# Last column group: the mean of the last token tile from summed weights, and a rearranged end

## Chip, cores and metric

The kernel runs on one core of a Trainium2 chip. The time is device time in microseconds (us) for one execution, as the median of several; the profile is that of one further execution. Engines are named as the profile does: PE is TensorE, DVE VectorE, ACT ScalarE, POOL GpSimd, SP SyncE, which issues the loads and stores here.

## What is computed

A two-layer decoder trunk over 256 tokens of width 2048: layer 0 is a gated recurrence, layer 1 a sparse attention with three branches. Only the end of layer 1 is touched:

```python
h = x
for i in range(DEPTH):
    ...
    h = _layer_norm(DEEPNORM_ALPHA * h + y, p[-2], p[-1])

def _layer_norm(x, g, b):
    mu = jnp.mean(xf, -1, keepdims=True)
    xc = xf - mu
    var = jnp.mean(xc * xc, -1, keepdims=True)
    return (xc * lax.rsqrt(var + LN_EPS) * g + b)
```

Here y is the product of the gated attention output (256 x 2048) with `l1_w_out` (2048 x 2048). For each token the mean and the variance go over all 2048 columns, so no output column is final before the last product of its row.

## The kernel before

All products are made with float32 values split into a high and a low part (`split`: ACT copies the high part in the reduced type, DVE subtracts it for the low part), three products for each pair of operands: high x high, high x low, low x high. `tok_step` issues these three for 128 tokens and one block of 128 of the 2048 inner rows; its lines are L146, L147 and L148 of the profile.

The output product runs over four groups of 512 columns, c = 0 to 3. The weights of a group come as eight blocks j0 to j7 of 256 inner rows (`load`, 512 KB each, issued by SP into one of four raw buffers `wr`; a buffer is free when its block has been split). `residual` adds ALPHA times the residual `xr` to the product in PSUM (`hb`, L860) and takes the statistics of 256 columns at a time (`stats`, L862). Residual and statistics of group c run while the weights of group c + 1 are split.

Groups 0 to 2 go through both token tiles block by block. The last group goes tile by tile (`project_by_tile`): first token tile 0 with all 512 columns, then tile 1, the last one, with two halves of 256 columns (`halve=True`), each with its own PSUM tile. After each tile `finish` runs: residual and statistics, then `moments` (aggregate L504, epsilon L505, and the power -0.5 on POOL, L232), then for each of four column quarters of 512 a centring (L876: subtract the mean, multiply by the gain) and a scaling (L878: multiply by 1/deviation, add the bias), and the store of the quarter (L879). `manual_schedule` keeps the order on DVE as written within this loop.

The order of everything else on the engines is set by a scheduler at build time, from priorities and its own estimate of the times: it is fixed in the program. So PE takes products of tile 1 in between those of tile 0 where the scheduler saw PE waiting for weights.

Of the kernel before, what the change touches and what calls it, by code (L numbers as in the profile page):

```python
# [8 lines left out]
F32 = mybir.dt.float32  # L9
F32R = mybir.dt.float32r  # L10
I32 = mybir.dt.int32
AF = mybir.ActivationFunctionType
OP = mybir.AluOpType
AX = mybir.AxisListType
# [3 lines left out]
D = 2048  # L18
S = 256
NT = S // 128  # L20
KT = D // 128
KG = KT // 4
DEPTH = 2
ALPHA = (2 * DEPTH) ** 0.25
# [7 lines left out]
AHEAD = 300  # L32
WARM = 8
PT = 2
HOLD = 7
# [20 lines left out]
def trunk(ctx, tc, a, out):  # L56
    nc = tc.nc
    pe, act, dve, pool = nc.tensor, nc.scalar, nc.vector, nc.gpsimd
    x = a["x"].rearrange("o s d -> (o s) d")
    xt = a["xT"].rearrange("(k p) s -> p k s", p=128)  # L60
    y = out.rearrange("o s d -> (o s) d")
# [9 lines left out]
    def pjb(shape):  # L71
        return pj.tile(shape, F32, name="pjb", tag="pjb")

    def mxb(shape):
        return mx.tile(shape, F32, name="mxb", tag="mxb")

    def split(hi, lo, src):

        act.activation(hi, src, AF.Copy)  # L79
        dve.tensor_tensor(lo, src, hi.bitcast(F32), op=OP.subtract)  # L80
# [22 lines left out]
    def load(w, j, c0, n):  # L103

        raw = slot([128, 2, n], F32, "wr", 3, 1)
        nc.sync.dma_start(raw, w[256 * j:256 * (j + 1), c0:c0 + n].rearrange("(k p) n -> p k n", p=128))
        return raw

    def weights(w, j, c0, n):
        return parts(load(w, j, c0, n))  # L110
# [7 lines left out]
    def widen():  # L118
        extra[0] = wide.enter_context(tc.tile_pool(name="wide", bufs=3, side="right"))
# [7 lines left out]
    def slot(shape, dtype, name, n, more):  # L127

        turn[name] = i = (turn.get(name, -1) + 1) % (n + more)
        p, b = (extra[0], more) if extra[0] and i >= n else (wts, n)  # L130
        if spare[0] and name == "wr" and extra[0] is None:

            spare[1] = i = (spare[1] + 1) % (n + SPARE)
            p, name, b = (spare[0], "ws", SPARE) if i >= n else (wts, name, n)
        return p.tile(shape, dtype, name=name, tag=name, bufs=b)

    def parts(raw):
        hi = slot(list(raw.shape), F32R, "wh", 5, 3)
        lo = slot(list(raw.shape), F32R, "wl", 5, 3)
        with tc.high_priority(AHEAD):  # L140
            split(hi, lo, raw)
        return hi, lo

    def tok_step(ps, xs, k, t, wh, wl):
        xh, xl = xs.at(k, slice(128 * t, 128 * (t + 1)))
        pe.matmul(ps, xh, wh, start=(k == 0), stop=False)  # L146
        pe.matmul(ps, xh, wl, start=False, stop=False)  # L147
        pe.matmul(ps, xl, wh, start=False, stop=(k == KT - 1))  # L148
# [10 lines left out]
                also(j)  # L159
        return ps  # L160

    def project_by_tile(xs, w, c0, after, behind=None, halve=False):


        ws = [weights(w, j, c0, 512) for j in range(KT // 2)]
        for t in range(NT):

            n = 256 if halve and t == NT - 1 else 512
            ps = []
            for c in range(0, 512, n):  # L170
                ps.append(pjb([128, n]))
                for k in range(KT):
                    hi, lo = ws[k // 2]
                    with tc.issue_after(behind) if behind and k >= HOLD else nullcontext():
                        tok_step(ps[-1], xs, k, t, hi[:, k % 2, c:c + n], lo[:, k % 2, c:c + n])
            behind = after(t, ps if len(ps) > 1 else ps[0])
        return behind

    def project_t(xs, w, c0, before=None, also=None):
# [20 lines left out]
    def transposed(src):  # L200

        ps = mxb([128, 4, 128])
        for i in range(4):
            last[0] = pe.transpose(ps[:, i], src[:, i], ident).ins  # L204
        return ps
# [6 lines left out]
    halves = consts.tile([128, 16], F32, name="halves")  # L212
# [18 lines left out]
    def rsqrt(o, v):  # L231
        pool.tensor_tensor(o, v, halves[:, :v.shape[1]], op=OP.pow)  # L232
# [88 lines left out]
    with tc.tile_pool(name="start", bufs=4) as start:  # L321
# [3 lines left out]
        ps = mxb([128, 128])  # L325
# [32 lines left out]
    oT = Pair("b")  # L358
# [116 lines left out]
    with tc.tile_pool(name="m0", bufs=1) as m0:  # L475
        ad = m0.tile([128, NT, 4, 128], F32, name="ad")
        pool.memset(ad, 0.0)
        for g in range(4):
            c0 = 512 * g
# [4 lines left out]
            v = m0.tile([128, NT, 512], F32, name="v")  # L484
# [16 lines left out]
    def moments(p, hb, stats, t):  # L501

        mv = p.tile([128, 4], F32, name="mv")
        dve.bn_aggr(mv[:, 0:2], stats[:, t])  # L504
        dve.tensor_scalar(mv[:, 2:3], mv[:, 1:2], LN_EPS, None, op0=OP.add)  # L505
        rsqrt(mv[:, 3:4], mv[:, 2:3])
        return mv

    hT = Pair("a")
    with tc.tile_pool(name="n0", bufs=2) as n0:  # L510
        hb = n0.tile([128, NT, D], F32, name="hb", bufs=1)
        stats = n0.tile([128, NT, 4, 6], F32, name="stats", bufs=1)
        for c in range(4):
            cs = slice(512 * c, 512 * (c + 1))
            xr = n0.tile([128, NT, 512], F32, name="xr")
            nc.gpsimd.dma_start(xr, x[:, cs].rearrange("(t p) d -> p t d", p=128))

            def residual(t, ps, c=c, cs=cs, xr=xr):
                dve.scalar_tensor_tensor(hb[:, t, cs], xr[:, t], ALPHA, ps, op0=OP.mult, op1=OP.add)
                dve.bn_stats(stats[:, t, c], hb[:, t, cs])  # L520

            def finish(t, ps):
                residual(t, ps)
                mv = moments(n0, hb, stats, t)
                for g in range(KG):
                    h = hb[:, t, 512 * g:512 * (g + 1)]
                    dve.tensor_scalar(h, h, mv[:, 0:1], mv[:, 3:4], op0=OP.subtract, op1=OP.mult)
                    ps = transposed(h.rearrange("p (k d) -> p k d", d=128))
                    h1 = n0.tile([128, 4, 128], F32, name="h1")
                    for k in range(4):  # L530
                        n = 4 * g + k
                        act.activation(h1[:, k], ps[:, k], AF.Identity, scale=g0c[:, n:n + 1],
                                       bias=b0c[:, n:n + 1])
                    hT.put(g, t, h1)
                nc.gpsimd.dma_start(norm0[128 * t:128 * (t + 1), :], hb[:, t])
                return last[0]
# [11 lines left out]
    oT = Pair("b")  # L548
# [79 lines left out]
    with tc.tile_pool(name="cmp", bufs=1) as cp:  # L628
# [38 lines left out]
        steps = []  # L667
# [16 lines left out]
        h = ck.hidden()  # L684
        ps = mxb([128, 4, NB])
# [9 lines left out]
        n = (512 + 48) // 2  # L695
        for t, ps in enumerate(project(hT, w1, C_VW, step, n=n)):
            split2(vals, (slice(None), t, 1, slice(0, n)), ps)
        h = cv.hidden()
# [5 lines left out]
        ps = mxb([128, 4, 128])  # L704
# [4 lines left out]
        ps = ps.rearrange("p g d -> p (g d)")  # L709
        for i in range(2):  # L710
            r, o = (slice(64 * b, 64 * b + 64) for b in (i, 1 - i))
# [111 lines left out]
    n1 = ctx.enter_context(tc.tile_pool(name="n1", bufs=2))  # L823
    hb = n1.tile([128, NT, D], F32, name="hb", bufs=1)
    stats = n1.tile([128, NT, 8, 6], F32, name="stats", bufs=1)
# [17 lines left out]
        return r  # L843


    for c in range(4):
        cs = slice(512 * c, 512 * (c + 1))

        xr = []

        def behind(j, c=c, xr=xr):
            if j == 3:
                xr.append(fetch(c))

        def residual(t, ps, c=c, xr=xr, parts=range(2)):
            xr = xr[0]
            n = ps.shape[1] // len(parts)
            for i, u in enumerate(parts):
                h = hb[:, t, 512 * c + 256 * u:512 * c + 256 * (u + 1)]
                dve.scalar_tensor_tensor(h, xr[:, t, 256 * u:256 * (u + 1)], ALPHA, ps[:, n * i:n * (i + 1)],  # L860
                                         op0=OP.mult, op1=OP.add)
                dve.bn_stats(stats[:, t, 2 * c + u], h)  # L862

        def finish(t, ps):
            if t:
                for u in range(2):
                    residual(t, ps[u], parts=(u,))
            else:
                residual(t, ps)
            mv = moments(n1, hb, stats, t)  # L870
            with tc.manual_schedule(engines={mybir.EngineType.DVE}):
                for g, half in ((0, 0), (0, 1), (1, 0), (1, 1), (2, 0), (2, 1), (3, 0), (3, 1)):
                    gs = slice(512 * g, 512 * (g + 1))
                    h = hb[:, t, gs]
                    if half == 0:
                        dve.scalar_tensor_tensor(h, h, mv[:, 0:1], g1[:, gs], op0=OP.subtract, op1=OP.mult)  # L876
                        continue
                    dve.scalar_tensor_tensor(h, h, mv[:, 3:4], b1[:, gs], op0=OP.mult, op1=OP.add)  # L878
                    nc.sync.dma_start(y[128 * t:128 * (t + 1), gs], h)  # L879

        if c < 3:
            for t, ps in enumerate(project(oT, a["l1_w_out"], 512 * c, behind)):
                residual(t, ps)
            if c == 2:
                last_xr = fetch(3)
            if c == 1:
                widen()
                g1, b1 = row("l1_ln_g"), row("l1_ln_b")
        else:
            xr.append(last_xr)  # L890
            project_by_tile(oT, a["l1_w_out"], 512 * c, finish, halve=True)
    wide.close()


# [31 lines left out]
```

## Time and profile before

| | us |
|---|---|
| median of 3 runs (1012.67 to 1014.42) | 1012.85 |
| the profiled execution | 1013.42 |
| its span, first to last instruction | 1011.7 |
| busy in the span: PE / DVE / ACT / POOL | 995.0 / 670.4 / 544.2 / 117.4 |

PE is busy 98% of the span, in matrix products that are issued one behind the other; a product's length in the timeline is longer than the distance to the next, because they overlap. For the distance between two operations compare their starts. All times in the rows are counted from the span's start.

### The profile page before, as it was taken

The numbers are of one execution on the slowest core, as the hardware profiler recorded it, in microseconds if no ns is written. First come the engines' busy times: TensorE is split into PE (matmuls) and PEld (weight loads), VectorE is DVE, ScalarE is ACT, GpSimd is POOL, SyncE is SP. The second block draws the span as 40 slices with busy tenths as digits, with TensorE's granted clock in tenths as the row PEclk, the third lists the DMA queues.
The fourth block names the chain that finished last, engine by engine and source line by source line (L and its number), as shares of the span: only waits on it lengthen the run. The fifth ranks groups of instructions, "written<-read, shape, count | busy, mean of one in ns | idle before, by whom it ended". The sixth has DMA issues, their size and how long they took to land.

```text
span 1011.7 us, 15913 instructions
## 1 busy us (share of the span) xinstructions
PE 995.0 (98%) x6041; PEld 883.0 (87%) x6041; DVE 670.4 (66%) x1101; ACT 544.2 (54%) x864; POOL 117.4 (12%) x180
## 2 busy tenths in 40 slices
PE   8999999999999999999999999999999999999995
PEld 8988998899889988888889888999989889998775
DVE  6796668656765677656575665555858568775566
ACT  6654455444544554434386655554857667774240
POOL 0400300030002000310011020101020022000540
PEclk9999999999999999999999999999999999999998
DMA  8875565556555665557466776666454455346962
GB/s 296 258 228 160 150 181 173 161 154 187 167 166 157 175 180 153 161 168 267 136 217 231 231 238 218 173 207 170 126 166 143 145 150 151 116 143 179 321 237 83
DMA packets 100780, 185.25 MB, mean 183 GB/s; under 512 B 6096, under 2 KB 20512, under 8 KB 100192
## 3 DMA queue, kind: packets, MB, share of 16 engines
q1 hardware_dynamic: 99232, 178.67, 57.4%
q0 software_dynamic: 1472, 5.56, 1.7%
q8 instruction: 47, 0.77, 0.3%
q14 instruction: 29, 0.24, 0.1%
HBM read 180.02 MB, written 4.19 MB: 182 GB/s over the span
## 4 chain that ended last, share of the span: by engine, by line
PE 91%; DMA 3%; DVE 2%; issue 1%; POOL 1%; SPq 0%; ACT 0%; POOLq 0%; DVEq 0%; ACTq 0%
PE pjb L147 17%; PE pjb L148 17%; PE pjb L146 17%; PE pjb L191 10%; PE pjb L193 10%; PE pjb L194 10%; PE mxb L431 2%; DMA wr<-in_l_w_out_dram 2%; PE mxb L204 1%; PE mxb L554 1%; PE mxb L556 1%; PE mxb L555 1%; PE mxb L785 1%; DVE wl L80 1%; DMA gb<-in_l_ln_g_dram 1%
## 5 line engine op out<-in xcount | busy, mean ns | idle before, releaser
L80 DVE TENSOR_TENSOR wl<-wr,wh 128x1024 fp32r<-128x1024 f32 (+2 forms) x305 | 369.5, 1217 | 197.8 <-ACT wh L79 195.8
L79 ACT ACTIVATE wh<-wr 128x1024 fp32r<-128x1024 f32 (+2 forms) x305 | 316.7, 1043 | 314.0 <-PE pjb L148 163.7
L191 PE MATMUL pjb<-ah,wh 128*128 128x256 f32 x832 | 236.0, 284 | 1.5 <-ACT wh L79 1.5
L193 PE MATMUL pjb<-al,wh 128*128 128x256 f32 x832 | 236.2, 285 | 0.0
L194 PE MATMUL pjb<-ah,wl 128*128 128x256 f32 x832 | 234.5, 284 | 0.5 <-DVE wl L80 0.5
L147 PE MATMUL pjb<-wl,ah 128*128 128x512 f32 (+1 forms) x576 | 222.6, 387 | 0.0
L146 PE MATMUL pjb<-wh,ah 128*128 128x512 f32 (+1 forms) x576 | 222.4, 387 | 0.0
L148 PE MATMUL pjb<-wh,al 128*128 128x512 f32 (+1 forms) x576 | 222.3, 386 | 0.0
L191 PEld LDWEIGHTS pjb<-ah,wh 128*128 128x128 f32 x832 | 157.4, 189 | 2.4 <-ACT wh L79 1.9
L194 PEld LDWEIGHTS pjb<-ah,wl 128*128 128x128 f32 x832 | 156.5, 189 | 0.9 <-DVE wl L80 0.7
L193 PEld LDWEIGHTS pjb<-al,wh 128*128 128x128 f32 x832 | 156.6, 188 | 0.5
L148 PEld LDWEIGHTS pjb<-wh,al 128*128 128x128 f32 x576 | 108.7, 189 | 22.2
L146 PEld LDWEIGHTS pjb<-wh,ah 128*128 128x128 f32 x576 | 108.7, 189 | 21.8
L147 PEld LDWEIGHTS pjb<-wl,ah 128*128 128x128 f32 x576 | 108.7, 189 | 21.3
L147 PE MATMUL pjb<-wl,bh 128*128 128x512 f32 (+1 forms) x272 | 105.1, 386 | 1.3 <-DVE wl L80 1.3
L148 PE MATMUL pjb<-wh,bl 128*128 128x512 f32 (+1 forms) x272 | 104.2, 384 | 0.0
L146 PE MATMUL pjb<-wh,bh 128*128 128x512 f32 (+1 forms) x272 | 103.2, 384 | 0.9 <-ACT wh L79 0.9
L147 PEld LDWEIGHTS pjb<-wl,bh 128*128 128x128 f32 x272 | 51.3, 189 | 13.7 <-DVE wl L80 3.1
L146 PEld LDWEIGHTS pjb<-wh,bh 128*128 128x128 f32 x272 | 51.1, 189 | 12.3 <-ACT wh L79 1.8
L148 PEld LDWEIGHTS pjb<-wh,bl 128*128 128x128 f32 x272 | 51.4, 189 | 10.4
L494 POOL TENSOR_TENSOR gz<-gz,gn 128x512 f32<-128x512 f32 x8 | 13.6, 1695 | 317.1 <-ACT gz L493 316.6
L80 DVE TENSOR_TENSOR wl<-ws,wh 128x1024 fp32r<-128x1024 f32 (+1 forms) x25 | 27.0, 1090 | 18.5 <-ACT wh L79 18.4
(222 smaller groups left out, 1047.4 us busy)
## 6 DMA issues: line engine op xcount, KB each, us to landing
wr<-in_l_w_in_dram SPq DMA_DIRECT2D x218, 512.0 KB, 3.8
wr<-in_l_w_out_dram SPq DMA_DIRECT2D x64, 512.0 KB, 4.4
ws<-in_l_w_in_dram SPq DMA_DIRECT2D x12, 512.0 KB, 4.5
wr<-in_l_cmp_w_k_dram SPq DMA_DIRECT2D x5, 512.0 KB, 3.9
wr<-in_l_cmp_w_v_dram SPq DMA_DIRECT2D x5, 512.0 KB, 3.8
wr<-in_l_w_in_dram SPq DMA_DIRECT2D x9, 280.0 KB, 3.1
xr<-in_x_dram POOLq DMA_DIRECT2D x4, 512.0 KB, 5.3
norm<-hb POOLq DMA_DIRECT2D x2, 1024.0 KB, 5.5
```

The lines of the kernel that those rows point to most:

```text
L79: act.activation(hi, src, AF.Copy)
L80: dve.tensor_tensor(lo, src, hi.bitcast(F32), op=OP.subtract)
L146: pe.matmul(ps, xh, wh, start=(k == 0), stop=False)
L147: pe.matmul(ps, xh, wl, start=False, stop=False)
L148: pe.matmul(ps, xl, wh, start=False, stop=(k == KT - 1))
L191: pe.matmul(o, hi[:, kk, c], xh, start=(k == 0 and b % 2 == 0), stop=False, skip_group_check=True)
L193: pe.matmul(o, hi[:, kk, c], xl, start=False, stop=False, skip_group_check=True)
L194: pe.matmul(o, lo[:, kk, c], xh, start=False, stop=(k == KT - 1), skip_group_check=True)
L204: last[0] = pe.transpose(ps[:, i], src[:, i], ident).ins
L431: pe.matmul(ps[:, h], km[:, h].rearrange("p b r j -> p (b r j)"), later, start=True, stop=True)
L494: pool.tensor_tensor(z, z, gn, op=OP.mult)
L554: pe.matmul(o, a[0], b[0], start=start, stop=False)
```

## The change

Three things are changed, all in the last column group.

The weights of this group get two more columns. For each block DVE sums the 256 columns of the second half (`tensor_reduce`, L864); the sum is split into high and low like the weights and stands, twice, behind the first half, so a row of a block is 256 + 2 + 256 columns with a stride of 258 between the halves. Token tile 0 reads the two halves as one operand of 2 x 256 columns; the last tile's first half reads 258 columns, its second 256. Column 256 of the first half's product is then the sum over the second half's columns of the product, one number for each token.

From it the mean of the last tile is known when its first half is done (`me`): the mean of the 1792 columns that are in `hb` by then (aggregate of seven statistics), the sum of the residual's last 256 columns, and the product's column 256.

With this mean the quarters are centred ahead of the variance: quarters 0 and 1 before the second half's residual, quarters 2 and 3 (the latter as two halves) behind `moments`' first two steps; then the four scalings and their stores follow. The variance is still that of `moments` over all eight statistics. Tile 0 is finished as before.

```diff
-    def project_by_tile(xs, w, c0, after, behind=None, halve=False):
+    def project_by_tile(xs, w, c0, after, behind=None, summed=None):
...
         for t in range(NT):
-
-            n = 256 if halve and t == NT - 1 else 512
...
+            if summed and t == NT - 1:
+                after(t, steps(pjb([128, 258]), t, 2), steps(pjb([128, 256]), t, 4))
+            else:
+                behind = after(t, steps(pjb([128, 512]), t, 0, behind))
         return behind
...
+    def summed(raw):
+
+
+        parts = [slot([128, 2, 516], F32R, name, 5, 3) for name in ("wh", "wl")]
+        ws = n1.tile([128, 2], F32, name="ws")
+        with tc.high_priority(AHEAD):
+            split(*(bass.AP(tensor=v.tensor, offset=v.offset, ap=[v.ap[0], [516, 2], [258, 2], [1, 256]])
+                    for v in parts), raw.rearrange("p k (u n) -> p k u n", u=2))
+            dve.tensor_reduce(ws, raw[:, :, 256:512], axis=AX.X, op=OP.add)
+            split(*(v[:, :, 256:258] for v in parts), ws[:, :, None].to_broadcast([128, 2, 2]))
...
+        def finish(t, ps, other=None):
...
+            known = D - 256
+            me = n1.tile([128, 6], F32, name="me", bufs=1)
+            dve.tensor_reduce(me[:, 0:1], xr[0][:, t, 256:512], axis=AX.X, op=OP.add)
             with tc.manual_schedule(engines={mybir.EngineType.DVE}):
...
+                residual(t, ps[:, 0:256], parts=(0,))
+                dve.scalar_tensor_tensor(me[:, 1:2], me[:, 0:1], ALPHA, ps[:, 256:257], op0=OP.mult, op1=OP.add)
+                dve.bn_aggr(me[:, 2:4], stats[:, t, 0:7])
+                dve.tensor_scalar(me[:, 4:5], me[:, 1:2], 1.0 / D, None, op0=OP.mult)
+                dve.scalar_tensor_tensor(me[:, 5:6], me[:, 2:3], known / D, me[:, 4:5], op0=OP.mult, op1=OP.add)
+                centred(t, me[:, 5:6], *quarters[0:2])
+                residual(t, other, parts=(1,))
+                mv = moments(n1, hb, stats, t)
+                centred(t, me[:, 5:6], quarters[2], (1536, known), (known, D))
+                scaled(t, mv[:, 3:4], *quarters)
```

The order of the instructions is the program's, engine by engine. First DVE where the weights of the last group are split. Before, from block j4 on (`wl_9810`) to j7 (`wl_9828`); `hb` and `stats` are residual and statistics of group c = 2:

```order
L80 TENSOR_TENSOR wl_9810<-wr_9807,wh_9809 128x1024
L860 SCALAR_TENSOR_TENSOR hb_9276<-xr_9685,pjb_9611 128x256 x2
L860 SCALAR_TENSOR_TENSOR hb_9276<-xr_9685,pjb_9612 128x256 x2
L80 TENSOR_TENSOR wl_9816<-wr_9813,wh_9815 128x1024
L862 BN_STATS stats_9277<-hb_9276 128x6 x4
L80 TENSOR_TENSOR wl_9822<-wr_9819,wh_9821 128x1024
L80 TENSOR_TENSOR wl_9828<-wr_9825,wh_9827 128x1024
```

In the changed kernel, the same place from the split of j4 (`wl_9826`) to that of j7 (`wl_9856`); `ws` are the sums:

```order
L80 TENSOR_TENSOR wl_9826<-wr_9823,wh_9825 128x4x256
L80 TENSOR_TENSOR wl_9816<-ws_9817,wh_9815 128x2x2
L887 SCALAR_TENSOR_TENSOR hb_9276<-xr_9685,pjb_9611 128x256 x2
L864 TENSOR_REDUCE ws_9827<-wr_9823 128x2
L887 SCALAR_TENSOR_TENSOR hb_9276<-xr_9685,pjb_9612 128x256 x2
L80 TENSOR_TENSOR wl_9836<-wr_9833,wh_9835 128x4x256
L864 TENSOR_REDUCE ws_9837<-wr_9833 128x2
L889 BN_STATS stats_9277<-hb_9276 128x6 x2
L80 TENSOR_TENSOR wl_9846<-wr_9843,wh_9845 128x4x256
L80 TENSOR_TENSOR wl_9826<-ws_9827,wh_9825 128x2x2
L889 BN_STATS stats_9277<-hb_9276 128x6 x2
L80 TENSOR_TENSOR wl_9856<-wr_9853,wh_9855 128x4x256
```

The sums of j4 and j5 stand ahead of the splits of j5 and j6; those of j6 and j7 follow behind the last split, ahead of the residual of token tile 0.

Second PE, at the first place where a product of the last tile is taken in between those of tile 0. Before (`pjb_9831` is tile 0, `pjb_9903` the last tile's first half) it stands behind the first product of j6:

```order
L146 MATMUL pjb_9831<-wh_9821,bh_5007 128x512
L146 MATMUL pjb_9903<-wh_9785,bh_5004 128x256
L147 MATMUL pjb_9903<-wl_9786,bh_5004 128x256
L148 MATMUL pjb_9903<-wh_9785,bl_5008 128x256
L146 MATMUL pjb_9903<-wh_9785,bh_5004 128x256
L147 MATMUL pjb_9903<-wl_9786,bh_5004 128x256
L147 MATMUL pjb_9831<-wl_9822,bh_5007 128x512
```

In the changed kernel (`pjb_9863` is tile 0, `pjb_9935` the first half with its two sums) it stands behind the first product of j5:

```order
L146 MATMUL pjb_9863<-wh_9835,bh_5006 128x512
L146 MATMUL pjb_9935<-wh_9785,bh_5004 128x258
L147 MATMUL pjb_9935<-wl_9786,bh_5004 128x258
L148 MATMUL pjb_9935<-wh_9785,bl_5008 128x258
L146 MATMUL pjb_9935<-wh_9785,bh_5004 128x258
L147 MATMUL pjb_9935<-wl_9786,bh_5004 128x258
L148 MATMUL pjb_9935<-wh_9785,bl_5008 128x258
L147 MATMUL pjb_9863<-wl_9836,bh_5006 128x512
```

Before, these five are all; in the changed kernel five more stand behind the first product of j6 and six behind that of j7, 17 together.

Third DVE at the end, from the last scaling of tile 0 on. Before:

```order
L878 SCALAR_TENSOR_TENSOR hb_9276<-hb_9276,mv_9884,l1_ln_b_9609 128x512
L860 SCALAR_TENSOR_TENSOR hb_9276<-xr_9774,pjb_9952 128x256
L862 BN_STATS stats_9277<-hb_9276 128x6
L504 BN_AGGR mv_10005<-stats_9277 128x2
L505 TENSOR_SCALAR mv_10005<-mv_10005 128x1
L876 SCALAR_TENSOR_TENSOR hb_9276<-hb_9276,mv_10005,l1_ln_g_9607 128x512
L878 SCALAR_TENSOR_TENSOR hb_9276<-hb_9276,mv_10005,l1_ln_b_9609 128x512
```

The last two rows come four times. In the changed kernel:

```order
L919 BN_AGGR me_10033<-stats_9277 128x2
L920 TENSOR_SCALAR me_10033<-me_10033 128x1
L899 SCALAR_TENSOR_TENSOR hb_9276<-hb_9276,mv_9916,l1_ln_b_9609 128x512
L921 SCALAR_TENSOR_TENSOR me_10033<-me_10033 128x1
L894 SCALAR_TENSOR_TENSOR hb_9276<-hb_9276,me_10033,l1_ln_g_9607 128x512 x2
L887 SCALAR_TENSOR_TENSOR hb_9276<-xr_9774,pjb_9984 128x256
L889 BN_STATS stats_9277<-hb_9276 128x6
L514 BN_AGGR mv_10047<-stats_9277 128x2
L515 TENSOR_SCALAR mv_10047<-mv_10047 128x1
L894 SCALAR_TENSOR_TENSOR hb_9276<-hb_9276,me_10033,l1_ln_g_9607 128x512
L894 SCALAR_TENSOR_TENSOR hb_9276<-hb_9276,me_10033,l1_ln_g_9607 128x256 x2
L899 SCALAR_TENSOR_TENSOR hb_9276<-hb_9276,mv_10047,l1_ln_b_9609 128x512 x4
```

The known mean and two centrings have moved ahead of the second half's residual (L887), the other centrings stand behind the epsilon (L515), and the four scalings come in a row.

## Rows read from the trace of the kernel before

**Rows 1.** Chain of waits of the whole span: shares of the engines.

```profile
PE 91%; DMA 3%; DVE 2%; issue 1%; POOL 1%; SPq 0%; ACT 0%; POOLq 0%; DVEq 0%; ACTq 0%
```

**Rows 2.** Stretches: length, busy PE, PEld, DVE, ACT, POOL, clock, DMA share, GB/s.

```profile
975.00:985.00 10.00, 9.16 (x37) 6.41 (x36) 8.69 (x13) 5.40 (x6) 0.68 (x1) 1.00 0.69 225
...
989.70:1000.40 10.70, 10.69 (x91) 10.48 (x89) 8.07 (x16) 0.00 (x0) 1.01 (x1) 1.00 0.26 99
1000.40:1008.10 7.70, 0.00 (x0) 0.00 (x0) 7.02 (x12) 0.00 (x0) 0.98 (x1) 0.67 0.25 97
1008.10:1011.70 3.60, 0.00 (x0) 0.00 (x0) 0.01 (x1) 0.00 (x0) 0.00 (x0) 0.50 0.22 85
```

**Rows 3.** Timeline of DVE behind the last product: start, length, operation, [idle before].

```profile
1000.43 0.42 DVE L860 SCALAR_TENSOR_TENSOR hb<-xr,pjb 128x256 f32<-128x256 f32 x1 [2.09 <-PE pjb L148]
...
1001.34 0.37 DVE L504 BATCH_NORM_AGGREGATE mv<-stats 128x2 f32<-128x48 f32 x1
1001.75 0.15 DVE L505 TENSOR_SCALAR mv<-mv 128x1 f32<-128x1 f32 x1
1001.82 0.74 DVE L876 SCALAR_TENSOR_TENSOR hb<-hb,mv,l_ln_g 128x512 f32<-128x512 f32 x1
1003.00 0.75 DVE L878 SCALAR_TENSOR_TENSOR hb<-hb,mv,l_ln_b 128x512 f32<-128x512 f32 x1 [0.44 <-POOL mv L232]
1003.67 0.75 DVE L876 SCALAR_TENSOR_TENSOR hb<-hb,mv,l_ln_g 128x512 f32<-128x512 f32 x1
1004.45 0.75 DVE L878 SCALAR_TENSOR_TENSOR hb<-hb,mv,l_ln_b 128x512 f32<-128x512 f32 x1
...
1007.35 0.75 DVE L878 SCALAR_TENSOR_TENSOR hb<-hb,mv,l_ln_b 128x512 f32<-128x512 f32 x1
```

**Rows 4.** Timeline of DVE at the splits of j1 to j4.

```profile
975.57 5.24 DVE L80 TENSOR_TENSOR wl<-wr,wh 128x1024 fp32r<-128x1024 f32 x4 [5.92 <-ACT wh L79]
```

**Rows 5.** Timeline of PE: a wait for a split, and the last two products.

```profile
983.33 0.50 PE L147 MATMUL pjb<-wl,bh 128*128 128x512 f32 x1 [0.61 <-DVE wl L80]
...
999.99 0.28 PE L147 MATMUL pjb<-wl,bh 128*128 128x256 f32 x1
1000.11 0.28 PE L148 MATMUL pjb<-wh,bl 128*128 128x256 f32 x1
```

**Rows 6.** Timeline of DVE at the end of token tile 0.

```profile
989.70 0.75 DVE L860 SCALAR_TENSOR_TENSOR hb<-xr,pjb 128x256 f32<-128x256 f32 x2 [1.67 <-PE pjb L148]
...
992.83 0.75 DVE L878 SCALAR_TENSOR_TENSOR hb<-hb,mv,l_ln_b 128x512 f32<-128x512 f32 x1 [0.46 <-POOL mv L232]
```

**Rows 7.** Timeline of DVE in the attention: a split, two reduces, a small operation.

```profile
841.26 1.23 DVE L80 TENSOR_TENSOR wl<-wr,wh 128x1024 fp32r<-128x1024 f32 x1 [0.70 <-ACT wh L79]
842.40 1.27 DVE L749 TENSOR_REDUCE st<-p 128x2 f32<-128x512 f32 x2
843.59 0.17 DVE L738 TENSOR_TENSOR p<-mxb,cmask 128x16 f32<-128x16 f32 x1
843.67 0.41 DVE L743 TENSOR_TENSOR p<-mxb,tri 128x256 f32<-128x256 f32 x1
```

**Rows 8.** ACT's groups by shape, a small one: busy us, mean ns, idle before.

```profile
L764 ACT ACTIVATE pcs<-p 128x64 fp32r<-128x64 f32 x16 | 3.8, 246 | 0.0
```

**Rows 9.** Timeline of PE in the attention: products of 272 columns.

```profile
842.72 0.29 PE L554 MATMUL mxb<-keys,qT 128*128 128x272 f32 x1
842.85 0.29 PE L555 MATMUL mxb<-keys,qT 128*128 128x272 f32 x1
```

**Rows 10.** Bytes moved in 40 slices of 1004.0 to 1011.7 us.

```profile
GB/s 0 0 0 266 426 372 287 11 0 0 74 372 415 383 117 0 0 0 245 404 404 298 11 0 0 74 362 372 426 128 0 0 0 0 0 0 0 0 0 0
```

**Rows 11.** The load of j7: issue, landing of such loads, ACT's copy.

```profile
979.52 0.37 SPq L106 DMA_DIRECT2D wr<-in_l_w_out_dram  x1
...
wr<-in_l_w_out_dram SPq DMA_DIRECT2D x8, 512.0 KB, 7.0
...
985.71 1.06 ACT L79 ACTIVATE wh<-wr 128x1024 fp32r<-128x1024 f32 x1 [0.27 <-DMA wr<-in_l_w_out_dram]
```

More of the change, by code (lines that the diff above doesn't have):

```diff
@@ L160, in project, with steps @@
         return ps
-    def project_by_tile(xs, w, c0, after, behind=None, halve=False):
-        ws = [weights(w, j, c0, 512) for j in range(KT // 2)]
-        for t in range(NT):
-            n = 256 if halve and t == NT - 1 else 512
[L169 to L176, printed above, removed]
+    def project_by_tile(xs, w, c0, after, behind=None, summed=None):
+        ws = []
+        for j in range(KT // 2):
+            if summed:
+                ws.append(summed(load(w, j, c0, 512)))
+            else:
+                hi, lo = weights(w, j, c0, 512)
+                ws.append([(hi[:, kk], lo[:, kk]) for kk in range(2)])
+        def steps(ps, t, i, behind=None):
+            for k in range(KT):
+                hi, lo = ws[k // 2][k % 2][i:i + 2]
+                with tc.issue_after(behind) if behind and k >= HOLD else nullcontext():
+                    tok_step(ps, xs, k, t, hi, lo)
+            return ps
+        for t in range(NT):
+            if summed and t == NT - 1:
+                after(t, steps(pjb([128, 258]), t, 2), steps(pjb([128, 256]), t, 4))
+            else:
+                behind = after(t, steps(pjb([128, 512]), t, 0, behind))
         return behind
@@ L843, in row, with halves @@
         return r
+    def summed(raw):
[6 more added lines that the diff above has]
+            split(*(v[:, :, 256:258] for v in parts), ws[:, :, None].to_broadcast([128, 2, 2]))
+        def halves(v, kk):
+            return bass.AP(tensor=v.tensor, offset=v.offset + 516 * kk, ap=[v.ap[0], [258, 2], [1, 256]])
+        return [[halves(v, kk) for v in parts] + [v[:, kk, 0:258] for v in parts] +
+                [v[:, kk, 258:514] for v in parts] for kk in range(2)]
     for c in range(4):
@@ L862, in residual, with centred @@
                 dve.bn_stats(stats[:, t, 2 * c + u], h)
[L864 to L868, printed above, removed]
-                residual(t, ps)
-            mv = moments(n1, hb, stats, t)
-            with tc.manual_schedule(engines={mybir.EngineType.DVE}):
[L872 to L879, printed above, removed]
+        def centred(t, m, *parts):
+            for a, b in parts:
+                h = hb[:, t, a:b]
+                dve.scalar_tensor_tensor(h, h, m, g1[:, a:b], op0=OP.subtract, op1=OP.mult)
@@ new lines, in scaled @@
+        def scaled(t, r, *parts):
+            for a, b in parts:
+                h = hb[:, t, a:b]
+                dve.scalar_tensor_tensor(h, h, r, b1[:, a:b], op0=OP.mult, op1=OP.add)
+                nc.sync.dma_start(y[128 * t:128 * (t + 1), a:b], h)
+        def finish(t, ps, other=None):
+            quarters = [(512 * g, 512 * (g + 1)) for g in range(4)]
+            if not t:
+                residual(t, ps)
+                mv = moments(n1, hb, stats, t)
+                with tc.manual_schedule(engines={mybir.EngineType.DVE}):
+                    for q in quarters:
+                        centred(t, mv[:, 0:1], q)
+                        scaled(t, mv[:, 3:4], q)
+                return
+            known = D - 256
+            me = n1.tile([128, 6], F32, name="me", bufs=1)
+            dve.tensor_reduce(me[:, 0:1], xr[0][:, t, 256:512], axis=AX.X, op=OP.add)
+            with tc.manual_schedule(engines={mybir.EngineType.DVE}):
+                residual(t, ps[:, 0:256], parts=(0,))
[5 more added lines that the diff above has]
+                residual(t, other, parts=(1,))
+                mv = moments(n1, hb, stats, t)
+                centred(t, me[:, 5:6], quarters[2], (1536, known), (known, D))
+                scaled(t, mv[:, 3:4], *quarters)
@@ L890, in trunk @@
             xr.append(last_xr)
-            project_by_tile(oT, a["l1_w_out"], 512 * c, finish, halve=True)
+            project_by_tile(oT, a["l1_w_out"], 512 * c, finish, summed=summed)
     wide.close()
```

## The prediction

> **What bounds the kernel now.** I read the chain of waits first. TensorE (PE) carries 91% of it [rows 1]; nothing upstream of the last column group is touched by the change, so only the tail matters. Next the stretches: until 1000.4 us PE is nearly full, then it has nothing left, and VectorE (DVE) alone works 7.7 us, followed by 3.6 us in which the last store lands and the program ends [rows 2]. The timeline of DVE shows what those 7.7 us are: residual and statistics of the last 256 columns (1000.43), aggregate (1001.34), epsilon (1001.75), and then four pairs "centre, scale", the first of which waits for GpSimd's power [rows 3]. Last, the stage before: the weights of the last group are split as they land (DVE 975.57, at the pace of ACT and the loads), and PE waits for them now and then, for instance 0.61 us at 983.33 [rows 4, 5]. So DVE has slack in that stage, but less than it seems: PE's idle time there is mostly a wait for DVE or for what feeds it.
>
> Names: j0 to j7 are the eight weight blocks of the last group, t0 and t1 its two token tiles; t1 is the last tile, t1a and t1b its column halves. R is the time at which DVE starts the residual of t0 (989.70 now), r1 that of the residual of t1b (1000.43 now).
>
> **What leaves the end.** After r1 DVE now needs 1000.43 to 1007.35 + 0.75 = 1008.10, that is 7.67 us [rows 3]. In the change, residual, statistics, aggregate and epsilon stay: 1000.43 to 1001.82, 1.39 us. Then come the centring of 512 and of twice 256 columns, and four scalings in a row. A 512-wide operation that does not need the one ahead starts 0.67 us behind it (1003.00 to 1003.67), one that does 0.78 us (1003.67 to 1004.45) [rows 3]; a 256-wide one takes 0.33 (0.75 for two, 0.42 for one) [rows 6, 3]. So the first scaling could start at 1.39 + 0.67 + 0.33 + 0.33 = 2.72 us. GpSimd's power is ready 1003.00 - 1001.75 = 1.25 us behind the epsilon [rows 3], at 1.32 + 1.25 = 2.57: hidden by 0.15 us behind the three centrings (without this cover it would still cost nothing, since the centrings end later). Scalings: 3 x 0.67 + 0.75 = 2.76. End at 5.48 us behind r1 instead of 7.67: **2.19 us less**, if r1 stays.
>
> [...]
>
> **What is added in front.** On DVE 22 operations more, all in the last group; on ACT eight small copies, between the block copies.
>
> First the weight stage. DVE's order for j2 to j7 becomes: sum over 512 numbers (tensor reduce), split of the block, small split of the two sums, and in between the residuals and statistics of the group before (four 256-wide operations of each kind, as now). j0's sum runs while the next loads are awaited, and j1's before its block is split (it needs the load alone, the split ACT's copy too), so both are hidden by the idle time ahead of 975.57, 5.92 us [rows 4]. From 975.57 on I add: seven splits x 1.14 (841.26 to 842.40) = 7.98; six sums x 0.595 (843.59 - 842.40 for two) = 3.57; seven small splits x 0.08 (843.59 to 843.67; the nearest is 16 wide, these are 4) = 0.56 [rows 7]; eight 256-wide x 0.33 = 2.64; the sum of the 256 residual columns 0.33. Together 15.08: DVE would be through at 990.65. The last sums go through ACT and back (a 64-wide ACT operation takes 0.246 us, a small split 0.17, and the reduce's own end trails by 0.08 [rows 7, 8]), so I add 0.4: **R = 991.05**, 1.35 later than now. The split reads and writes rows that are 258 apart instead of one run of 1024; no row shows that, I take it at nothing (the upper bound is two operations of 512 for one of 1024, 7 x 0.2 = 1.4 us).
>
> ACT keeps up: eight times 0.25 more in a stage where it stands idle between loads. PE can't go ahead of this: its second product of each block needs DVE's low half. But its order puts 17 products of t1a where it now has 5 (the order stands with the change), 12 x 0.119 = 1.43 us that fill the longer waits; t0 then ends at about 990.9, and what is left of t1, 79 products, takes 79 x 0.119 = 9.4 us. The work of PE is the same but for 48 x 2 columns: 272 columns take 0.13 (842.72 to 842.85) [rows 9], 256 take 0.119, so 48 x 0.001 = 0.05 us. I keep PE's end at 1000.4 (last product at 1000.11 [rows 5]), with 0.3 either way.
>
> Then from R to r1. Now: R to the first scaling 992.83 - 989.70 = 3.13 [rows 6]. In the change the same 3.13, and until r1 nine 512-wide operations (four scalings and three centrings of t0, two centrings of t1) x 0.67 = 6.03, residual and statistics of t1a 2 x 0.33 = 0.66, and the known mean: an aggregate (0.37) and three one-column operations, 0.37 + 3 x 0.07 + some 0.1 for waits among them = 0.65 (1001.34 to 1001.75 to 1001.82 [rows 3]). Sum 10.47: **r1 = 991.05 + 10.47 = 1001.52**, 1.1 us after PE is done. Before, DVE reached this place early and waited for PE; now PE waits for nobody and DVE is late. That is the cost: 1.1 of the 2.19 us.
>
> DVE ends at 1001.52 + 5.48 = 1007.0 instead of 1008.10: **-1.1 us**. The four stores of t1 then follow each other at 0.67 instead of 1.45 us. The bytes of a store move in a burst of about 0.83 us (four to five slices of 7.7 / 40 = 0.19 us, the full ones at 370 to 430 GB/s) [rows 10]; 262 KB at 390 GB/s need 0.67, so between nothing and 3 x 0.16 = 0.5 us of queueing. I take 0.1, because the rate within a burst matches the pace. What follows DVE's end, 3.6 us [rows 2], stays. The profiled execution took 1013.42 (span 1011.7 and 1.7 around it); the sum gives 1012.4 for it, and as it lies 0.57 above the median of 1012.85 shown, **1012.85 - 1.0 = 1011.9**.
>
> **Rivals.**
> - *DVE is not late.* If the weight stage and the known mean cost 1.1 us less than my sum, r1 waits for PE again at 1000.43 and the whole 2.19 comes, less 0.1 for stores: 1010.75. For it: the splits might overlap better than 1.14. Against: every price is a measured pitch, and the small splits have ACT in their loop.
> - *The gain is eaten by a late load.* The load of j7 goes out when DVE is through with j3: 979.52 now, about 980.7 then, since three sums stand ahead (behind it on SP's queue stand only the stores, which come much later). It is landed when ACT starts on it, 985.71, 6.2 us later; the median of these loads is 7.0 [rows 11]. With 6.2 it lands at 986.9, ACT's copy ends at 988.0, and DVE comes to it at 988.1: just covered. It decides from 7 us on; at 8 us R moves by 1.7 and the sum is +0.7: 1013.5. The same result comes if the strided split costs its upper bound (+0.4: 1013.2). Together this case is 1012.6 to 1013.9, a gain not to be seen.
> - *Slower: TensorE dislikes the new operands.* t0's products read two runs of 256 columns with a gap, t1a's read 258 columns. If 258 columns took two passes, 2 x 0.119, 48 products would cost 5.8 us more, PE would end at 1006.2, and DVE 5.48 later: +3.6, 1016.4. It decides for slower (over 0.2%) when PE ends 4.2 us later, 0.04 us on each of 96 products. Against: 272 and 256 columns stand in proportion [rows 9, 5].
>
> **How the numbers follow.** 0.2% is 2.0 us, about what a measurement of this kernel tells from no change. The forecast (1011 to 1012.5): 0.58. DVE not late: 0.11, of which some lies below 1010.8. Late load or split: 0.23. Slow operands: 0.08. Faster by over 0.2% 0.10, within 0.82, slower 0.08. The range leaves out the slow operands and the fringe of the best case: 1010.8 to 1013.6.
>
> **What the new profile would show.** Right: DVE without a gap from about 976 to the end; its residual of t0 at 991 +- 0.5; the residual of t1b over 0.8 us after PE's last product; 5.5 us from there to DVE's end, with no wait for GpSimd; stores 0.67 apart. Wrong: DVE waiting for PE at r1 (best case), for ACT or a load in 980 to 989 (late load), or 258-wide products more than 0.125 us apart.

## The result and the profile after

| | before | after |
|---|---|---|
| median, us (6 runs each) | 1013.02 (1012.67 to 1014.42) | 1005.55 (1005.22 to 1006.60) |
| ratio, 95% interval | | 0.993 [0.992, 0.994] |
| the profiled execution | 1013.42 | 1005.65 |
| its span | 1011.7 | 1003.9 |

The change gains 7.5 us where 1.0 was forecast; 1005.55 lies well below the range of 1010.8 to 1013.6. The end of the program went nearly as the prediction had it, but began 7 us earlier. First the page of the changed kernel, its head and the busy times:

```profile
span 1003.9 us, 15938 instructions
...
PE 988.1 (98%) x6041; PEld 877.3 (87%) x6041; DVE 675.4 (67%) x1123; ACT 545.3 (54%) x872; POOL 118.1 (12%) x180
```

DVE has 22 operations and 5.0 us more, as the change says. PE has the same 6041 products and 6.9 us less (995.0 before). Nothing in the diff shortens a product; the last group's are even a little wider.

The prediction named the timeline of DVE as its test; here it is, in the weight stage and behind it:

```profile
968.74 1.23 DVE L80 TENSOR_TENSOR wl<-wr,wh 128x1024 fp32r<-128x1024 f32 x1 [0.49 <-ACT wh L79]
...
982.39 1.27 DVE L864 TENSOR_REDUCE ws<-wr 128x2 f32<-128x512 f32 x2
983.58 0.15 DVE L80 TENSOR_TENSOR wl<-ws,wh 128x4 fp32r<-128x4 f32 x1
983.93 0.17 DVE L80 TENSOR_TENSOR wl<-ws,wh 128x4 fp32r<-128x4 f32 x1 [0.20 <-ACT wh L79]
984.19 0.75 DVE L887 SCALAR_TENSOR_TENSOR hb<-xr,pjb 128x256 f32<-128x256 f32 x2
...
994.47 0.41 DVE L887 SCALAR_TENSOR_TENSOR hb<-xr,pjb 128x256 f32<-128x256 f32 x1
...
995.85 1.53 DVE L894 SCALAR_TENSOR_TENSOR hb<-hb,me,l_ln_g 128x512 f32<-128x512 f32 x3
997.30 2.73 DVE L899 SCALAR_TENSOR_TENSOR hb<-hb,mv,l_ln_b 128x512 f32<-128x512 f32 x4
```

And PE's last product:

```profile
993.33 0.28 PE L148 MATMUL pjb<-wh,bl 128*128 128x256 f32 x1
```

The reader is to see two things. From one row to the next the distances are the forecast ones: 15.45 us from j1's split to R (968.74 to 984.19), 10.28 from R to r1 (994.47), 5.56 from r1 to the end of the four scalings (997.30 + 2.73); no wait for POOL ahead of the scalings, where [rows 3] has one of 0.44. But the first of these rows stands 6.83 us ahead of its place in [rows 4] (975.57).

So I went upstream, to a load that stands ahead of the last groups in SP's queue, before and after:

```profile
931.62 1.41 SPq L842 DMA_DIRECT2D l_ln_b<-in_l_ln_b_dram  x1
```

```profile
924.57 1.39 SPq L852 DMA_DIRECT2D l_ln_b<-in_l_ln_b_dram  x1
```

It goes out 7.05 us earlier, though every instruction ahead of it is the same in the same order. What follows it takes 80.1 us before (1011.7 - 931.62) and 79.3 after. So **7 of the 7.8 us between the two spans came from a part of the program that the diff doesn't touch.** Two stretches show how. Each reaches from one product to another, the same two in both kernels; the first has 238 products of 256 columns between the starts, the second 224 of 512 (the count in the row includes one or two more at the edges). The rows are those of stretches: length, busy time of PE, clock, DMA share, GB/s. Before, and after:

```profile
230.41:258.96 28.55, 28.55 (x240) 1.00 0.64 185
448.93:501.40 52.47, 52.47 (x225) 1.00 0.62 201
```

```profile
228.46:256.77 28.31, 28.31 (x240) 1.00 0.62 186
445.45:497.58 52.13, 52.13 (x226) 1.00 0.61 202
```

PE waits for nothing in either and has its full clock. Yet the pitch of the products, from one start to the next (length by 238 and by 224), is 120.0 ns before and 118.9 after with 256 columns, 234.2 and 232.7 with 512. At the first stretch the changed kernel is 1.95 us ahead, at the second 3.48, at the load above 7.05: the gain grows over the whole program. What the change does to all of it is one thing: a buffer of a tag in a tile pool is as large as the largest tile asked of that tag, and the last group's `wh` and `wl` ask for 2x516 elements. So every buffer of the split weights in the main pool (`wts`; for most of the program an extra pool, `wide`, adds three buffers of each tag) takes 4128 bytes of a partition in place of 4096, from the first instruction on, and all these tiles lie elsewhere.

### The profile page after: what moved, and what is told of

Same layout as the page of the kernel before. It is cut to its first block, busy times and chain, and to the rows that moved or that the text cites. A ratio compares the mean times of both kernels' runs of the same rounds, so it can differ in the third digit from the quotient of the medians.

```text
span 1003.9 us, 15938 instructions
## 1 busy us (share of the span) xinstructions
PE 988.1 (98%) x6041; PEld 877.3 (87%) x6041; DVE 675.4 (67%) x1123; ACT 545.3 (54%) x872; POOL 118.1 (12%) x180
## 3 DMA queue, kind: packets, MB, share of 16 engines
q0 software_dynamic: 1472, 5.56, 1.7%
## 4 chain that ended last, share of the span: by engine, by line
PE 90%; DMA 4%; DVE 3%; POOL 1%; issue 1%; ACT 1%; SPq 0%; DVEq 0%; POOLq 0%
PE pjb L146 16%; PE pjb L148 16%; PE pjb L147 16%; PE pjb L201 10%; PE pjb L204 10%; PE pjb L203 10%; PE mxb L441 2%; DMA wr<-in_l_w_out_dram 2%; DMA gb<-in_l_ln_g_dram 1%; PE mxb L214 1%; PE mxb L564 1%; PE mxb L565 1%; PE mxb L566 1%; PE mxb L795 1%; DVE wl L80 1%; PE mxb L614 1%
## 5 line engine op out<-in xcount | busy, mean ns | idle before, releaser
L147 PE MATMUL pjb<-wl,bh 128*128 128x512 f32 (+2 forms) x272 | 104.5, 385 | 2.2 <-DVE wl L80 1.9
L148 PE MATMUL pjb<-wh,bl 128*128 128x512 f32 (+2 forms) x272 | 103.6, 382 | 0.0
L146 PE MATMUL pjb<-wh,bh 128*128 128x512 f32 (+2 forms) x272 | 102.6, 383 | 0.3 <-ACT wh L79 0.3
L80 DVE TENSOR_TENSOR wl<-ws,wh 128x1024 fp32r<-128x1024 f32 (+2 forms) x33 | 28.2, 863 | 18.4 <-ACT wh L79 18.2
```

## Experiments

In the kernel before, the allocation puts all split-weight tiles at 480 past a multiple of 512 bytes, 4096 apart, and the activations that they are multiplied with (`ah`, `al`, `bh`, `bl`) at 64. In the changed kernel the main pool's split weights lie at 160 to 448, each 32 past the one before, and the extra pool's nearly all at 160. The operands of nearly all products start a multiple of 512 bytes into their tiles, so these numbers hold for them as well. The distance below is from the activations' place to the weights': 416 before.

The medians of before in the three rounds of runs were 1012.14, 1012.85 and 1012.65 us; each kernel is compared with that of its own round.

**The larger buffers alone (e1).**

```diff
-    def parts(raw):
-        hi = slot(list(raw.shape), F32R, "wh", 5, 3)
-        lo = slot(list(raw.shape), F32R, "wl", 5, 3)
+    def parts(raw, room=None):
+        hi = slot(room or list(raw.shape), F32R, "wh", 5, 3)
+        lo = slot(room or list(raw.shape), F32R, "wl", 5, 3)
+        if room:
+            hi, lo = (bass.AP(tensor=v.tensor, offset=v.offset, ap=[v.ap[0], [512, 2], [1, 512]])
+                      for v in (hi, lo))
...
-        ws = [weights(w, j, c0, 512) for j in range(KT // 2)]
+        ws = [parts(load(w, j, c0, 512), [128, 2, 516] if halve else None) for j in range(KT // 2)]
```

> The kernel before, with one edit: the split weights of the last group ask for a tile of 2x516 elements and use 2x512 of it in one piece. No instruction is added, moved or changed in shape; but each buffer of the two split-weight tags of the main weight pool takes 4128 bytes of a partition in place of 4096, so these tiles lie at other addresses in the whole program. Theory A (the start address of a split-weight tile sets how fast TensorE works through it: 32 bytes past a multiple of 64 is slower than on it; before, all tiles are 32 past, with 4128-byte buffers about half are on it): about 1006, some 6.9 below the kernel before, and the moment of j1's split already 6.8 earlier, as in the changed kernel. Theory B (the 7 us come with the change's own instructions or from something at the start): 1013, no difference. Theory C (what counts is the distance between tiles, 4096 bytes, at which buffers that are read and written together fall on each other): about 1006 too.

Measured: 1005.72 us, ratio 0.9934 [0.9922, 0.9947]. The same two stretches:

```profile
228.63:256.95 28.32, 28.32 (x241) 1.00 0.63 186
445.62:497.75 52.13, 52.13 (x225) 1.00 0.62 202
```

The lengths are those of the changed kernel to 0.01 us. Theory B falls: 6.4 of the gain come without one of the change's operations. (The executions of one kernel differ by some tenths at these places, so e1 and after are told apart only at the end; more on that under e9.)

**Which addresses? Two tries at alignment (e2, e3, e4).** e2 and e4 are the changed kernel with buffers of 4160 bytes, e4 also with the unused tiles of e3:

```diff
-        parts = [slot([128, 2, 516], F32R, name, 5, 3) for name in ("wh", "wl")]
+        parts = [slot([128, 2, 520], F32R, name, 5, 3) for name in ("wh", "wl")]
+        parts = [bass.AP(tensor=v.tensor, offset=v.offset, ap=[v.ap[0], [516, 2], [1, 516]])
+                 for v in parts]
```

e3 is the kernel before, with 32 unused bytes on either side of the split weights of each pool:

```diff
-        return p.tile(shape, dtype, name=name, tag=name, bufs=b)
+        if name == "wh" and (id(p), 0) not in gap:
+            gap[id(p), 0] = p.tile([128, 8], F32, name="gap0", tag="gap0", bufs=1)
+        v = p.tile(shape, dtype, name=name, tag=name, bufs=b)
+        if name == "wl" and (id(p), 1) not in gap:
+            gap[id(p), 1] = p.tile([128, 8], F32, name="gap1", tag="gap1", bufs=1)
+        return v
```

> The changed kernel, with buffers of 4160 bytes in place of 4128 (2x520 elements asked for, the same 2x516 used): every split-weight tile is again 32 bytes past a multiple of 64, as in the kernel before, but the distance between tiles isn't 4096. Theory A: the 6.9 us are gone and only the change of the tail is left, 1012.0 (1011.5 to 1012.6). Theory B: 1005.6. Theory C: 1005.6 or a little lower.

> The kernel before, with two unused tiles of 32 bytes in each of the two weight pools, one ahead of and one behind the split weights: every split-weight tile starts on a multiple of 64 bytes, 4096 apart as before; every other tile keeps its place against 64 bytes. Theory A: about twice the gain of the changed kernel's addresses, since there each pair of high and low parts had one of the two on a multiple of 64: 995 to 1001, with the 512-wide products at about 230 ns in place of 234 and the 256-wide ones at about 118 in place of 121. Theories B and C: 1013, no difference.

> The changed kernel with buffers of 4160 bytes and the same unused tiles of 32 bytes: every split-weight tile starts on a multiple of 64 bytes. Theory A: 1.0 us under the kernel before with the same addresses, so 994 to 1000. Theory B and theory C: 1005.6.

Measured: e2 1008.98 (0.9971 [0.9960, 0.9981]), e3 1003.55 (0.9911 [0.9898, 0.9925]), e4 1006.94 (0.9948 [0.9936, 0.9961]). None is where theory A put it, and theory C misses e3. For e2 and e4 the median misleads: with these sizes the scheduler also puts products of t1a ahead of t0's in the last group, and t0's residual waits for PE. In e2:

```profile
988.52 0.75 DVE L889 SCALAR_TENSOR_TENSOR hb<-xr,pjb 128x256 f32<-128x256 f32 x2 [3.66 <-PE pjb L148]
```

Up to the load named above e2 is 6.6 us ahead of before, though all its split weights stand 32 past a multiple of 64: theory A is wrong. e3 keeps the 4096 between tiles and gains 8.6: theory C is wrong. But e3 held a hint. Its extra pool came to lie at 384, its main pool at 448, and products with the extra pool's tiles took 114.6 ns (256 columns) and 229.6 (512) against 118.9 and 232.5 with the main pool's (means over all products of the trace, each put to its tile by its turn in the program); in the kernel before the two pools are within 0.5 ns of each other.

**Place, or distance between two places (e5 to e8, e12).** All five have the instructions of the kernel before in the same order on every engine; only unused bytes are added. e5, e7, e8 and e12 move the split weights (`above` is 96, 64, 224 and 160; in e7 the second line ends in `else 64`), e6 moves the activations instead. The edits of e5 and of e6:

```diff
+        above = 96
+        below = 512 - above if p is wts else -above % 64
+        if name == "wh" and (id(p), 0) not in gap:
+            gap[id(p), 0] = p.tile([128, below // 4], F32, name="gap0", tag="gap0", bufs=1)
...
+            gap[id(p), 1] = p.tile([128, above // 4], F32, name="gap1", tag="gap1", bufs=1)
```

```diff
+    consts.tile([128, 24], F32, name="gap")
+
     def pjb(shape):
```

> The kernel before, with the same instructions in the same order on every engine; unused tiles of 96 bytes behind the split weights (and others ahead of them) put every split-weight tile 96 bytes lower, at 384 past a multiple of 512 (before: 480; in e3: 448 in the main pool, 384 in the extra one; the activations' tiles lie at 64). In e3 the products with the extra pool's tiles had 229.6 ns (512 wide) and 114.6 (256 wide), those with the main pool's 232.5 and 118.9. Theory A (a multiple of 64 is all that counts): as e3, 1003.5. Theory D (the place within 512 bytes counts, of the weights by themselves): all products as those of e3's extra pool, so 2171 x 4.5 ns + 2513 x 5.3 = 23 us under the kernel before, about 990. Theory E (the distance from the weights' place to that of the activations, 320, counts): about 990 too.

> The kernel before, with the same instructions in the same order; an unused constant of 96 bytes moves the activations' tiles (and all else on that side) 96 bytes up, from 64 to 160 past a multiple of 512; the weights stay at 480. The distance between the two is that of e5. Theory A: no difference, 1012 to 1013. Theory D: no difference. Theory E: as e5, about 990.

> As e5, but 64 bytes lower than before: 416 past a multiple of 512, so 32 past a multiple of 64 as in the kernel before. Theory A: no difference, 1012 to 1013. Theories D and E: between e3's main pool and e5 if the time falls evenly with the place, about 997; they fix no value.

> As e5, but 224 bytes lower than before: 256 past a multiple of 512, a multiple of 64. In e4 the extra pool's first tiles lay there, with 233.2 and 117.8 ns. Theory A: as e3, 1003.5. Theories D and E: 2171 x 0.95 + 2513 x 2.2 = 7.6 us under the kernel before, about 1005.

> As e5, but 160 bytes lower than before: the split weights lie at 320 past a multiple of 512, 256 from the activations' place at 64. Theory E (the distance within 512 bytes sets the pace) fixes no value for a distance that wasn't run; distances of 320, 352, 384 and 416 gave 995, 1007, 1003 and 1013, 192 gave 1005. If the time were a smooth dip around 320, about 1000.

Measured, with the pitch of the products worked out from the same two stretches:

| | weights at | activations at | distance | us | ratio | 256 columns, ns | 512 columns, ns |
|---|---|---|---|---|---|---|---|
| before | 480 | 64 | 416 | 1012.1 to 1012.9 | 1 | 120.0 | 234.2 |
| e3 | 448, extra pool 384 | 64 | 384, 320 | 1003.55 | 0.9911 | 116.9 | 231.1 |
| e7 | 416 | 64 | 352 | 1007.09 | 0.9944 [0.9930, 0.9957] | 117.3 | 233.3 |
| e5 | 384 | 64 | 320 | 994.92 | 0.9822 [0.9809, 0.9836] | 117.8 | 228.9 |
| e6 | 480 | 160 | 320 | 995.52 | 0.9832 [0.9819, 0.9845] | 117.8 | 228.9 |
| e12 | 320 | 64 | 256 | 999.35 | 0.9870 [0.9855, 0.9885] | 120.0 | 226.9 |
| e8 | 256 | 64 | 192 | 1004.77 | 0.9920 [0.9906, 0.9933] | 117.8 | 233.3 |

The stretches of e5 and of e6:

```profile
225.53:253.56 28.03, 28.03 (x240) 1.00 0.63 188
440.42:491.69 51.27, 51.27 (x225) 1.00 0.64 206
```

```profile
225.69:253.73 28.04, 28.04 (x241) 1.00 0.62 188
440.58:491.86 51.28, 51.28 (x226) 1.00 0.64 205
```

and of e12:

```profile
227.54:256.09 28.55, 28.55 (x240) 1.00 0.61 185
442.60:493.43 50.83, 50.83 (x225) 1.00 0.62 207
```

e6 decides. Its weights lie where they lay before; the activations, and all else on their side of the memory, have moved, and it gains what e5 gains, to 0.01 us in either stretch. From the first stretch to the second, 215 us, the two traces stay 0.16 us apart. Theories A and D forecast no difference for e6; E is the one that stands: **what changed the pace is where the two operands of the products lie relative to each other.** The weights' own place doesn't do it, and their distance from one another, the same 4096 bytes in all these runs, isn't needed for it. e7 adds that no multiple of 64 is needed (5.8 us gained at 352). e12 adds that the two kinds of products don't agree: at a distance of 256 the 512-wide ones are faster still (226.9 ns), the 256-wide ones as slow as before (120.0). In the 512-wide ones the weights stream past loaded activations, in the 256-wide ones the other way round. e12 at 999.35 met its loose forecast of about 1000, e8 (1004.77) its forecast of about 1005; for e7 it was 997, which missed by 10: the dip isn't smooth.

The distance isn't all. Ahead of the two stretches stands one in which e5 and e6 differ: the same 143 products of 256 columns between the starts, in e5 and in e6:

```profile
36.31:52.52 16.21, 16.21 (x146) 1.00 0.78 252
```

```profile
35.87:52.71 16.84, 16.84 (x146) 1.00 0.76 248
```

That is 113.4 ns in e5 and 117.8 in e6, at one distance, with no wait and the full clock in both. So 256-wide products have two paces at a distance of 320. The table's 117.8 is the slower one; over the whole program they average 116.2 in e5 and 116.5 in e6. What picks between the two no run shows. It bears on the forecast of e5, 5 us too good: that took the 114.6 of e3's extra pool, close to the faster pace, for all 256-wide products, and e5 has the faster pace in parts of the program only.

**The end by itself (e9, e10, e11).** e9 is the changed kernel, e10 is e1 again; both have the same places for the weights' buffers, and differ by what the change was written for.

> The changed kernel once more, beside e10, which has the same addresses of the split weights and the old end. If the end of the program is as forecast (the change worth 1.0 us there), 1.0 us under e10; if the later start of the residual takes back more than forecast (the traces of the changed kernel and of e1 have their ends 0.3 us apart), 0.3 under e10.

> The kernel of e1 once more, on the same chip as e9: about 1005.7 to 1006.5, by 0.3 to 1.0 over e9.

Measured: e9 1004.98 (1004.50 to 1005.26), e10 1006.23 (1005.57 to 1007.59), 1.25 us apart with ranges that don't touch. In its own round each kernel with the old end is 6.42 under the kernel before (e1 and e10), the changed one 7.47 and 7.67. So by the medians the end is worth 1.0 to 1.3, about what was forecast, though a measurement of this kernel can hardly tell 0.8 from 1.6 here. The profiled executions, one of each, don't settle it: the span of e1 is 0.3 longer than that of the changed kernel (1004.2 and 1003.9), e10's 3.1 longer than e9's. The rows of e1 show where: the residual of t0, that of t1b, and the end of DVE.

```profile
982.20 0.75 DVE L863 SCALAR_TENSOR_TENSOR hb<-xr,pjb 128x256 f32<-128x256 f32 x2 [1.66 <-PE pjb L151]
...
992.91 0.42 DVE L863 SCALAR_TENSOR_TENSOR hb<-xr,pjb 128x256 f32<-128x256 f32 x1 [2.06 <-PE pjb L151]
...
999.84 0.75 DVE L881 SCALAR_TENSOR_TENSOR hb<-hb,mv,l_ln_b 128x512 f32<-128x512 f32 x1
```

With the faster products the old kernel reaches R at 982.20, waiting for PE; the changed one is there at 984.19, late by DVE's own work, and waits no more. From r1 on e1 needs 7.68 us (992.91 to 1000.59), the changed kernel 5.56.

e11 takes the row sums from DVE:

```diff
-            split(...)
-            dve.tensor_reduce(ws, raw[:, :, 256:512], axis=AX.X, op=OP.add)
+            for kk in range(2):
+                act.activation(hi[:, kk, 1], src[:, kk, 1], AF.Copy, accum_out=ws[:, kk:kk + 1])
+            act.activation(hi[:, :, 0], src[:, :, 0], AF.Copy)
+            dve.tensor_tensor(lo, src, hi.bitcast(F32), op=OP.subtract)
```

> The changed kernel with the row sums of the weights taken by ScalarE, which adds them up in the copy that makes the high part (the half that is summed is copied by two instructions of their own). Theory T (the eight reductions of about 0.6 us make VectorE late in the weight stage, so that the last half's residual starts 0.85 us behind the last product): VectorE is rid of 4.8 us there, waits for TensorE at both residuals, and the end comes 0.85 us earlier than in e9. Rival (VectorE's lateness isn't the bound, or ScalarE's longer chain makes the split weights late): no gain on e9, or a loss.

Measured: 1004.57 (1004.06 to 1004.72), 0.4 under e9 with ranges that overlap: not settled by the times. The rows of DVE at R, at r1 and at the four scalings:

```profile
982.86 0.75 DVE L891 SCALAR_TENSOR_TENSOR hb<-xr,pjb 128x256 f32<-128x256 f32 x2 [1.46 <-PE pjb L148]
...
993.56 0.42 DVE L891 SCALAR_TENSOR_TENSOR hb<-xr,pjb 128x256 f32<-128x256 f32 x1
...
996.41 2.73 DVE L903 SCALAR_TENSOR_TENSOR hb<-hb,mv,l_ln_b 128x512 f32<-128x512 f32 x4
```

DVE waits for PE at R again, and r1 comes 0.03 us behind PE's last product (993.25 + 0.28), where the changed kernel has 0.86. Theory T is right about the lateness; of the 0.85 us that it promised, the median shows half at most. The traces show more: from the load above to DVE's end it is 74.4 us in e11 (924.75 to 999.14), 75.1 in e9 (923.88 to 998.95) and 75.5 in the first trace of the changed kernel, one execution each.

## Why the prediction was wrong, and where it was right

**The step that failed** stands at the start of its reasoning: "nothing upstream of the last column group is touched by the change, so only the tail matters". No instruction upstream was touched, but every split-weight tile was, by 32 bytes more per buffer. That is worth 6.4 us by e1's median and 7 by the moment of one load, nearly the whole result; the forecast put it at nothing, and no rival had it. The prediction looked at the order of instructions and the diff of the code; the line that counted was `slot([128, 2, 516], ...)`, read together with `tag=name` in `slot`.

**What leaves the end**: 5.48 us behind r1 forecast, 5.56 measured, with POOL's power hidden as said. Right.

**The weight stage on DVE**: 15.08 + 0.4 forecast from j1's split to R, 15.45 measured. The strided split was taken at nothing, and its upper bound of 1.4 us isn't in the rows: 968.74 with 1.23 is the length of [rows 7]. Right.

**R to r1**: 10.47 forecast, 10.28 measured; r1 stands 0.86 behind PE's end (993.61) where 1.1 was forecast. Right, 0.2 us too dear (the terms for the known mean add up to 0.68, not 0.65).

**R itself, 1.35 later than before**: mis-sized. Against e1, which has the same places of the weights, it is 2.0 later (984.19 and 982.20). Of the 0.65 more, 0.4 is that e1 needs only 13.74 us from j1's split (968.46) to R where the kernel before needs 14.13; that its faster products bring PE to t0's end sooner, while DVE's work is no shorter, is the likely reason. The rest is that j1's split itself starts 0.28 later than in e1. PE's own end is 0.74 later than e1's (993.61 and 992.87), where "I keep PE's end" was said, with 0.3 either way.

**The stores**: 3.87 us from DVE's end to the end of the span (1003.9 - 1000.03), 0.27 more than the 3.6 of [rows 2], where 0.1 was taken.

The sum was -1.0. e9 against e10 gives -1.25, but the two traces with their rows here give less: r1 comes 1.56 us later than in e1 (994.47 and 992.91) instead of 1.1, DVE ends 0.56 earlier, and with the stores 0.3 is left. So two of its terms, R and PE's end, were off, and that the medians agree with the sum may in part be luck. Of the rivals, a late load didn't come (the only wait in DVE's rows between j1's split and R is 0.20 for ACT), and TensorE didn't dislike the new operands: with 258 columns the products follow each other at a median of 0.119 us. That rival asked for the right thing, a different pace of PE through its operands, but only in 96 products of the last group and only for the worse.

On PE's operands the Trainium skill ("TensorE: Matmul & The Clock Gate", section "Step-by-step: what each phase is for") says that the engine has two independent read ports, and that loading the next stationary operand takes no bandwidth from the running product. By that one would not expect the place of the one against the other to matter. In the runs it does: 234.2 ns at one distance, 226.9 at another, with the same instructions. The measurement decides on the pace; whether the loading is what costs, the runs don't show.

**What stays open.** That the load of the next stationary operand and the streaming one meet in the memory is a likely reading, since the distance of just these two counts, but only argued: no run took the loads away. That the distance counts within 512 bytes wasn't separated from other spans either. Nor does the distance of a product's own operands give its pace where the buffers lie at several distances: in the changed kernel the 512-wide products whose weights lie at a distance of 320 have 231.5 ns on average, in e5, where all lie there, 229.5. So the 7 us of the change itself are shown to come from the places (e1), but aren't worked out from the distances. And the end of the changed kernel wasn't run at a distance of 320: its 514 columns don't fit the buffers of 4096 bytes that keep all weights at one place.

## What to carry to other kernels

Before calling a change local, look at what it does to tile sizes: one larger tile in a shared tag moves every tile of that tag, and a kernel that is full of matrix products can change by a per cent with no instruction touched. To find such a thing, lay one early and one late instruction of both traces side by side; if the shift grows evenly, the pace has changed, not a place. And the placement is worth trying for itself: moving one kind of operand by 96 bytes took 17 to 18 us from this kernel (e5, e6), more than twice what the change did.

## Not expected of the hardware

- The pitch of products with a full TensorE clock (granted 1.00, that is 2.4 GHz) and no wait went from 234.2 to 226.9 ns (512 columns, e12) and from 120.0 to 116.9 (256 columns, e3) through the place of their operands alone.
- The distance between the two operands counts: moving either by 96 bytes had the same effect (28.03 and 28.04 us, 51.27 and 51.28 us in the two stretches).
- One distance can have two paces: the same 143 products of 256 columns took 113.4 ns each in e5 and 117.8 in e6.
- The best distance isn't the same when the roles of the operands are exchanged: 256 is the best of those tried for 512-wide products and among the two worst for 256-wide ones.
